# A matmul that reads its moving columns in turns from two halves

## The chip, the cores and the metric

The kernel runs on one core of one Trainium2 chip. The metric is the device time of one execution, in microseconds. Before the change the median of three runs is 925.33 us (925.14 to 925.72).

## The reference

One layer of a hybrid decoder block, float32, 512 tokens of 1024 channels. In short:

```
h    = RMSNorm(x);  proj = h @ w_in              # 1024 x 9216
y_a  = (B * conv3(C * v)) @ w_a_out              # B, C, v, u, ug, q, gates: columns of proj
y_b  = silu(LN(conv31(u * sigmoid(ug)))) @ w_b_out
y_c  = attention(q, RMSNorm(mem) @ w_kv) @ w_att_out     # 4 heads, 256 memory tokens
x    = x + (sum_i sigmoid(gate_i) * y_i) @ w_o
h2   = RMSNorm(x);  gt, up = split(conv3(h2 @ w_up))     # 1024 x 5632, causal, per channel
out  = RMSNorm(x + (silu(gt) * up) @ w_down)             # 2816 x 1024
```

The convolutions run along the tokens, each token using its predecessors.

## The kernel before, in words

Every product is made of three float32r matmuls: each operand is split into a high part (a ScalarE cast, line 495 for weights) and a low part (VectorE, line 499), and hi·hi, hi·lo and lo·hi are added up in PSUM.

The two large projections, `h @ w_in` and `h2 @ w_up`, go by quads. A quad makes 512 output channels (two tiles of 256) for all 512 tokens, by a Strassen-like scheme with seven products in place of eight: sums and differences of weight blocks (made by adding DMAs of GpSimd, line 633, or VectorE) meet sums and differences of the activations (`OPERAND`: b00, b10, b11, t4 to t7), which are kept as ready-split tiles of 128 partitions x 4 x 256 tokens. There are 18 quads in the mixer and 11 in the feed-forward part.

`multiply(q, f, act)` issues one product: 24 matmuls on line 675, two halves of 128 output channels, four blocks of 128 input channels, three terms each. The stationary operand is 128 x 128 of a weight, the moving one `a[k]`, 256 columns (tokens) that lie side by side. The result of 2 x 256 columns fills one PSUM bank. `quad_reads` empties the banks: `r1`, `r5`, `r6`, `r4` are ScalarE copies (r4 with a factor of -1), `r2`, `r7`, `r3` VectorE additions or subtractions into the quad's two output tiles `first` and `second`. In r5 the tile takes +b; in r7 `minus(t, x, y)` computes -x - y, so that -(a + b) stands there.

The other matmuls are not quads: keys (line 929, also 256 columns), attention, the merges of the three branches (lines 1417 to 1419), `w_o` and `w_down` (`product`, lines 446 to 448, mostly 512 columns).

The order of the work is planned when the program is built. `Jobs` holds every step as a job with an engine, a cost in us and what it needs. TensorE's jobs run in a list written out by hand. The jobs of ScalarE, VectorE, SP (weight loads) and GpSimd (adding DMAs) are put in order by a greedy clock that adds up the costs, with due times reckoned back from TensorE's list and corrections by hand (`LATER`, `AHEAD`). `MM`, `MM_HALF` and `MM_QUAD` in line 419 are the costs of a matmul of 512 columns, of 256 columns in some places, and of a quad's or a key's matmul; a product of a quad is booked at 24 x `MM_QUAD`. The engines then work through their own queues in that order, with semaphores between them. Weights pass through rings: six landing buffers `wf` and four pairs `whi`, `wlo`.

Of the kernel before, what the change touches and what calls it, by code (L numbers as in the profile page):

```python
# [10 lines left out]
AF = mybir.ActivationFunctionType  # L11
ALU = mybir.AluOpType
# [319 lines left out]
def hybrid_block_kernel(  # L332
# [19 lines left out]
    nc = tc.nc  # L352
# [27 lines left out]
    job = jobs.add  # L380
# [3 lines left out]
    def make(key, dtype=F32):  # L384

        ring, i = jobs.place[key]
        label = "_".join(str(k) for k in key) if isinstance(key, tuple) else key
        if ring == "ps":
            t = psum.tile([P, SEQ], F32, tag=f"ps{i}", name=name(str(key[0])))
        elif ring == "wf":  # L390
            t = wts.tile([P, 1024], F32, tag=f"wf{i}", name=name("wf"), bufs=1)
        else:
            t = places[ring].tile([P, 1024], dtype, tag=f"{ring}{i}", name=name(str(key[0])))
        tiles[key] = t
        return t

    def two(key):

        return tiles[key].rearrange("p (c n) -> p c n", c=2)
# [4 lines left out]
    def halves(key):  # L404

        return tiles[key].rearrange("p (c n) -> p c n", c=2)


    def dve(n):
        return (n + 151) / 960.0 - 0.08  # L410

    def actv(n):
        return (n + 224) / 1200.0 - 0.08
# [2 lines left out]
        return n / 1160.0 + 0.175 + extra  # L416

    TAP = 0.665
    MM, MM_HALF, MM_QUAD = 0.2268, 0.12, 0.1142
    LOAD, MORE, MORE_WIDE = 1.42, 2.55, 2.55  # L420
    LOAD_LATENCY, MORE_LATENCY = 3.1, 3.4

# [6 lines left out]
    cols, at = {}, 0  # L429
# [4 lines left out]
    def par(key, i):  # L434
        return pk[:, cols[key] + i : cols[key] + i + 1]
# [3 lines left out]
    nc.scalar.preload_act_table_set("sqrt_and_others")  # L439
    nc.scalar.dma_start(out=pk[:, :N_GAINS], in_=packed[:, :N_GAINS])  # L440
    nc.scalar.copy(mean_w, mean_col.broadcast_to([P, P]))

    def product(ps, w_hi, w_lo, s_hi, s_lo, start, stop, again=False):


        nc.tensor.matmul(ps, s_hi, w_hi, start=start, stop=False, skip_group_check=again)  # L446
        nc.tensor.matmul(ps, s_hi, w_lo, start=False, stop=False, skip_group_check=again)  # L447
        nc.tensor.matmul(ps, s_lo, w_hi, start=False, stop=stop, skip_group_check=again)  # L448

    def minus(t, x, y):  # L450

        nc.vector.scalar_tensor_tensor(t, x, -1.0, y, op0=ALU.mult, op1=ALU.subtract)
# [102 lines left out]
    lo_t, hi_t = slice(0, HALF), slice(HALF, SEQ)  # L555
# [107 lines left out]
    def multiply(q, f, act):  # L663
        if f in (1, 2, 5):
            make(("bank", q, BANK_OF[f]))
        ps = halves(("bank", q, BANK_OF[f]))
        (w_hi, w_lo), (hi, lo) = w_units.pop((q, f)), form[act, OPERAND[f]]
        for c in range(2):
            at = slice(c * P, (c + 1) * P)
            for i in range(4):  # L670
                k = 3 - i if f == 4 and c else i
                first = f in (1, 2, 5) and i == 0 and c == 0
                again = not (f in (1, 2, 5) and c == 0)
                for n, (w, a) in enumerate(((w_hi, hi), (w_hi, lo), (w_lo, hi))):
                    nc.tensor.matmul(  # L675
                        ps[:, c, :], w[:, k, at], a[k], start=first and n == 0,
                        stop=i == 3 and n == 2, skip_group_check=again,
                    )

    def multiply_job(q, f, act, unit=True):  # L680
        bank = ("bank", q, BANK_OF[f])
        after = [("wl", (q, f))]
        if (act, OPERAND[f]) in form_ready:
            after += form_ready[act, OPERAND[f]]
        else:
            after.append(("fl", act, OPERAND[f]))
        after += {6: [("r1", q)], 7: [("r6", q)], 4: [("r7", q)], 3: [("r5", q)]}.get(f, [])
        pe((q, f), 24 * MM_QUAD, lambda: multiply(q, f, act), after,
           take=[(bank, "ps")] if f in (1, 2, 5) else [], use=[] if f in (1, 2, 5) else [bank],
           unit=unit)  # L690
# [3 lines left out]
    def quad_reads(q, first, second, ring, after=()):  # L694

        f, s = lambda: two(first), lambda: two(second)
        bank = lambda b: ("bank", q, b)
        view = lambda b: halves(bank(b))

        def read1():  # L700
            make(first)
            nc.scalar.copy(f()[:, :, lo_t], view("a"))

        def read5():
            make(second)
            nc.scalar.copy(s()[:, :, hi_t], view("b"))

        def add(t, b):
            nc.vector.tensor_tensor(t, t, b, op=ALU.add)

        job(("r1", q), "ACT", actv(512), read1, [(q, 1)] + list(after),
            take=[(first, ring)], use=[bank("a")])
        job(("r2", q), "DVE", dve(512), lambda: add(f()[:, :, lo_t], view("c")),
            [(q, 2), ("r1", q)], use=[bank("c"), first])
        job(("r5", q), "ACT", actv(512), read5, [(q, 5)] + list(after),
            take=[(second, ring)], use=[bank("b")])
        job(("r6", q), "ACT", actv(512), lambda: nc.scalar.copy(f()[:, :, hi_t], view("a")),
            [(q, 6), ("r1", q)], use=[bank("a"), first])
        job(("r7", q), "DVE", dve(512), lambda: minus(s()[:, :, hi_t], view("a"), s()[:, :, hi_t]),
            [(q, 7), ("r5", q)], use=[bank("a"), second])  # L720
        job(("r3", q), "DVE", dve(512), lambda: add(f()[:, :, hi_t], view("b")),
            [(q, 3), ("r6", q)], use=[bank("b"), first])
        job(("r4", q), "ACT", actv(512), lambda: nc.scalar.activation(
            s()[:, :, lo_t], view("a"), AF.Copy, scale=-1.0), [(q, 4), ("r5", q)],
            use=[bank("a"), second])

    def ready_of(q, second):
# [307 lines left out]
    def mixer_quad(q, first, second, col0, col1):  # L1035
        quad_loads(q, w_in, col0, col1, by_dma=q != ("glu", 0), take=("wf+" + ANY, 6))
        quad_reads(q, first, second, ANY)
# [4 lines left out]
    for i in range(2):  # L1042
        a, b = 2 * i, 2 * i + 1
# [7 lines left out]
    for h in range(HEADS):  # L1051
# [18 lines left out]
        for tp in range(2):  # L1070
            at = ATT + 12 * h + 6 * tp
# [313 lines left out]
    for p in range(4):  # L1385
# [5 lines left out]
            lambda k, j, p=p: par("conv_a_w", k * KC + 2 * p + j), [("CV", p), ("ldp",)], ANY,  # L1391
# [347 lines left out]
    for q in range(QUADS):  # L1739
        up = ("up", q)  # L1740
        quad_loads(up, w_up, q * 256, D_FF + q * 256, by_dma=True,
                   **({"take": ("wf lf",), "after": [("fl", "h2", "t4")]} if 2 < q < 9 else {}))
        quad_reads(up, ("gt", q), ("uu", q), "tm",
                   ["temps"] + ([("z", q - 2)] if q > 1 else []))
        for value, src, acc in ((0, ("gt", q), ("gtc", q)), (1, ("uu", q), ("upc", q))):
            conv3_jobs(
                ("cf", q, value), src, acc,
                lambda k, j, q=q, v=value: par(
                    "conv_ffn_w", k * 2 * FC + v * FC + 2 * q + j),
                ready_of(up, value) + ([("z", q - 1)] if q else []), "tm",  # L1750
            )
        job(("silu", q), "ACT", actv(1024) + (0 if q else TABLE), lambda q=q: nc.scalar.activation(
            tiles["gtc", q], tiles["gtc", q], AF.Silu), [(("cf", q, 0), "done")],
            use=[("gtc", q)])
        job(("z", q), "DVE", dve(1024), lambda q=q: gated(q),
            [("silu", q), (("cf", q, 1), "done")], use=[("gtc", q), ("upc", q)])
# [112 lines left out]
    first = [(UP[0], 1), (UP[0], 2), "tr2", (UP[1], 1), "tr3", (UP[1], 2), (UP[2], 1), (UP[0], 5), (UP[2], 2), (UP[0], 6), (UP[1], 5), (UP[0], 7), (UP[0], 3), (UP[0], 4), (UP[1], 6), (UP[2], 5), (UP[1], 7), (UP[2], 6), (UP[1], 4), (UP[1], 3)]  # L1869
# [62 lines left out]
    for g, ps in enumerate(PIECES):  # L1932
        n = (ps.stop - ps.start) * HALF
        here = [("z", ps.stop - 1)]
        job(("zd", g), "DVE", dve(n), lambda ps=ps: z_difference(ps), here)
        for p, at in (("a", (0, 0)), ("b", (0, 1)), ("d", (0, 1)), ("c", (0, 0)), ("e", (0, 0)),
# [12 lines left out]
            k = down_pieces.index((p, g)) - 3  # L1949
# [46 lines left out]
    for u, ps in enumerate(PAIR_UNITS):  # L1996
        n = ps.stop - ps.start
# [239 lines left out]
```

## Time and profile before

| | |
|---|---|
| median of the runs | 925.33 us |
| span of the profiled execution | 923.8 us |
| TensorE matmuls | 916.6 us busy, 99%, 6677 matmuls |
| VectorE | 837.4 us, 91% |
| ScalarE | 671.0 us, 73% |
| GpSimd | 126.5 us, 14% |
| mean granted TensorE clock | 0.999 |

The page gives the span, from the first to the last instruction; the profiled execution has no other time of its own in it, and the runs' median lies 1.5 us above it. In the profile PE is TensorE, PEld its weight loads, DVE VectorE, ACT ScalarE, POOL GpSimd. Matmuls overlap in the pipeline, so the length of one (some 278 ns for 256 columns) is longer than the distance from one to the next; a busy TensorE does not say at which pace it works. The chain is followed back from the last instruction, at each step to what released it.

### The profile page before, as it was taken

What the parts mean: (1) busy time and instruction counts of PE and PEld (TensorE: products, weight loads), DVE (VectorE), ACT (ScalarE), POOL (GpSimd) and SP (SyncE); (2) the same over time, 40 slices, a digit from 0 to 9 for tenths busy, and PEclk for the clock granted to TensorE, in tenths of its full rate; (3) what the DMA queues carried; (4) which work ended last, traced back from release to release, by engine and by line L of the source; (5) the groups of instructions that cost most, each with busy time, mean ns of one, the idle gap of its engine ahead of it and who ended that gap; (6) DMA issues with size and microseconds to landing.
All of it is one profiled execution on the core that took longest, in us unless ns stands there. A gap on an engine that the chain in (4) does not pass through costs nothing.

```text
span 923.8 us, 16764 instructions
## 1 busy us (share of the span) xinstructions
PE 916.6 (99%) x6677; PEld 862.8 (93%) x6677; DVE 837.4 (91%) x953; ACT 671.0 (73%) x911; POOL 126.5 (14%) x153
## 2 busy tenths in 40 slices
PE   9999999999999999999999999999999999999997
PEld 8999999999989999999899888899999999988886
DVE  6897999989989999999986779898999889999987
ACT  7567988879977887788746743777766676765656
POOL 0121121101111211110100001021221121003300
PEclk9999999999999999999999999999999999999999
DMA  9999689666787879788956598499999877789962
GB/s 364 367 252 199 151 178 205 167 160 137 194 188 205 183 168 213 174 210 201 220 108 173 157 322 187 114 227 307 279 248 226 207 142 149 197 266 338 244 131 92
DMA packets 54366, 190.60 MB, mean 206 GB/s; under 512 B 6160, under 2 KB 6544, under 8 KB 54288
## 3 DMA queue, kind: packets, MB, share of 16 engines
q0 software_dynamic: 20880, 75.24, 45.2%
q1 hardware_dynamic: 33120, 114.02, 34.7%
q8 instruction: 52, 0.85, 0.3%
q10 hardware_dynamic: 288, 0.27, 0.1%
q14 instruction: 26, 0.21, 0.1%
HBM read 185.31 MB, written 4.19 MB: 205 GB/s over the span
## 4 chain that ended last, share of the span: by engine, by line
PE 95%; DMA 2%; DVE 1%; issue 0%; ACT 0%; POOL 0%; DVEq 0%; POOLq 0%; ACTq 0%
PE bank L675 57%; PE bank L448 7%; PE bank L446 7%; PE bank L447 7%; PE bank L1418 5%; PE bank L1417 5%; PE bank L1419 5%; PE bank L929 2%; DMA wf<-in_w_up 2%; PE bank L1766 0%; PE ss L802 0%; DVE wlo L499 0%; PE bank L1166 0%; DVE upc L1373 0%; DVE gtc L1373 0%
## 5 line engine op out<-in xcount | busy, mean ns | idle before, releaser
L495 ACT CAST whi<-wf 128x1024 fp32r<-128x1024 f32 (+1 forms) x199 | 206.9, 1044 | 97.7 <-PE bank L675 39.3
L499 DVE TENSOR_TENSOR wlo<-wf,whi 128x1024 fp32r<-128x1024 f32 (+1 forms) x193 | 232.4, 1211 | 29.8 <-ACT whi L495 29.6
L1238 ACT ACTIVATE tp<-u,pk 128x510 f32<-128x510 f32 (+22 forms) x184 | 119.4, 704 | 7.0 <-DVE acc L1245 6.9
L1245 DVE TENSOR_TENSOR acc<-acc,tp 128x1020 f32<-128x1020 f32 (+22 forms) x92 | 109.2, 1188 | 6.0 <-ACT tp L1238 5.0
L633 POOL DMA_DIRECT2D wf<-in_w_in x51 | 45.1, 890 | 245.1 <-DVE wlo L499 160.2
L675 PE MATMUL bank<-ft6h,wlo 128*128 128x256 f32 x232 | 64.3, 277 | 0.1
L675 PE MATMUL bank<-fb10h,whi 128*128 128x256 f32 x232 | 64.4, 278 | 0.0
L675 PE MATMUL bank<-fb00h,whi 128*128 128x256 f32 x232 | 64.4, 278 | 0.0
L675 PE MATMUL bank<-ft6h,whi 128*128 128x256 f32 x232 | 64.4, 277 | 0.0
L675 PE MATMUL bank<-ft7h,whi 128*128 128x256 f32 x232 | 64.3, 277 | 0.0
L675 PE MATMUL bank<-ft7l,whi 128*128 128x256 f32 x232 | 64.3, 277 | 0.0
L675 PE MATMUL bank<-ft7h,wlo 128*128 128x256 f32 x232 | 64.3, 277 | 0.0
L675 PE MATMUL bank<-fb00l,whi 128*128 128x256 f32 x232 | 64.3, 277 | 0.0
L675 PE MATMUL bank<-fb11h,whi 128*128 128x256 f32 x232 | 64.3, 277 | 0.0
L675 PE MATMUL bank<-fb00h,wlo 128*128 128x256 f32 x232 | 64.3, 277 | 0.0
L675 PE MATMUL bank<-ft5h,wlo 128*128 128x256 f32 x232 | 64.3, 277 | 0.0
L675 PE MATMUL bank<-ft5h,whi 128*128 128x256 f32 x232 | 64.3, 277 | 0.0
L675 PE MATMUL bank<-ft5l,whi 128*128 128x256 f32 x232 | 64.3, 277 | 0.0
L675 PE MATMUL bank<-ft6l,whi 128*128 128x256 f32 x232 | 64.2, 277 | 0.0
L675 PE MATMUL bank<-fb10h,wlo 128*128 128x256 f32 x232 | 64.2, 277 | 0.0
L675 PE MATMUL bank<-fb10l,whi 128*128 128x256 f32 x232 | 64.2, 277 | 0.0
L675 PE MATMUL bank<-fb11l,whi 128*128 128x256 f32 x232 | 64.1, 276 | 0.0
(388 smaller groups left out, 3146.1 us busy)
## 6 DMA issues: line engine op xcount, KB each, us to landing
wf<-in_w_in SPq DMA_DIRECT2D x55, 512.0 KB, 5.1
wf<-in_w_in POOLq DMA_DIRECT2D x51, 512.0 KB, 6.2
wf<-in_w_up SPq DMA_DIRECT2D x29, 512.0 KB, 5.7
wf<-in_w_up POOLq DMA_DIRECT2D x28, 512.0 KB, 6.1
wf<-in_w_down SPq DMA_DIRECT2D x15, 512.0 KB, 3.7
wf<-in_w_att_out SPq DMA_DIRECT2D x8, 512.0 KB, 4.5
wf<-in_w_a_out SPq DMA_DIRECT2D x8, 512.0 KB, 4.2
wf<-in_w_b_out SPq DMA_DIRECT2D x8, 512.0 KB, 4.3
```

The lines of the kernel that those rows point to most:

```text
L446: nc.tensor.matmul(ps, s_hi, w_hi, start=start, stop=False, skip_group_check=again)
L447: nc.tensor.matmul(ps, s_hi, w_lo, start=False, stop=False, skip_group_check=again)
L448: nc.tensor.matmul(ps, s_lo, w_hi, start=False, stop=stop, skip_group_check=again)
L495: nc.scalar.copy(parts[0], src())
L499: nc.vector.tensor_tensor(lo, src(), hi.bitcast(F32), op=ALU.subtract)
L633: nc.gpsimd.dma_start(out=tiles[key], in_=block(w, col[c], k), accum_op=ALU.add)
L675: nc.tensor.matmul(ps[:, c, :], w[:, k, at], a[k], start=first and n == 0, stop=i == 3 and n == 2, skip_group_check=again,)
L1238: nc.scalar.activation(two(("tp", p, s))[:, j, s:], two(("u", p))[:, j, : SEQ - s], AF.Copy, scale=weight(j),)
L1245: nc.vector.tensor_tensor(a, a, two(("tp", p, s))[:, :, s:], op=ALU.add)
L1417: nc.tensor.matmul(ps, w_hi[:, i, at], hi, start=first, stop=False)
L1418: nc.tensor.matmul(ps, w_hi[:, i, at], lo, start=False, stop=False)
L1419: nc.tensor.matmul(ps, w_lo[:, i, at], hi, start=False, stop=last)
```

## The change

The matmuls of the quads read their 256 columns in the order 0, 128, 1, 129, and so on: `in_turns` views the operand as two halves and takes a column from each in turn. The bank then holds the columns in that order, and its seven readers view it with `turned` (columns two apart, first the even ones, then the odd ones) and their tiles in SBUF with `parted` (two runs of 128), so that every token stands again where it stood. The readers' view needs one step more than the helper `minus` is given, so r7 becomes a plain subtraction, s - a, and r5 takes its bank with a factor of -1 in its place. The planner's cost of a quad's matmul is put at 0.1119 where it was 0.1142; the keys' matmuls, whose reading isn't changed, are booked at the same number.

```
-    MM, MM_HALF, MM_QUAD = 0.2268, 0.12, 0.1142
+    MM, MM_HALF, MM_QUAD = 0.2268, 0.12, 0.1119
...
+    def in_turns(t):
+        return t.rearrange("p (a b) -> p b a", a=2)
+
+    def turned(t):
+        if len(t.shape) == 3:
+            return t.rearrange("p c (b a) -> p c a b", a=2)
+        return t.rearrange("p (b a) -> p a b", a=2)
+
+    def parted(t):
+        if len(t.shape) == 3:
+            return t.rearrange("p c (a b) -> p c a b", a=2)
+        return t.rearrange("p (a b) -> p a b", a=2)
...
                     nc.tensor.matmul(
-                        ps[:, c, :], w[:, k, at], a[k], start=first and n == 0,
+                        ps[:, c, :], w[:, k, at], in_turns(a[k]), start=first and n == 0,
...
         def read1():
             make(first)
-            nc.scalar.copy(f()[:, :, lo_t], view("a"))
+            nc.scalar.copy(parted(f()[:, :, lo_t]), turned(view("a")))
         def read5():
             make(second)
-            nc.scalar.copy(s()[:, :, hi_t], view("b"))
+            nc.scalar.activation(
+                parted(s()[:, :, hi_t]), turned(view("b")), AF.Copy, scale=-1.0)
-        def add(t, b):
-            nc.vector.tensor_tensor(t, t, b, op=ALU.add)
+        def add(t, b, op=ALU.add):
+            nc.vector.tensor_tensor(parted(t), parted(t), turned(b), op=op)
...
-        job(("r6", q), "ACT", actv(512), lambda: nc.scalar.copy(f()[:, :, hi_t], view("a")),
+        job(("r6", q), "ACT", actv(512), lambda: nc.scalar.copy(
+            parted(f()[:, :, hi_t]), turned(view("a"))),
...
-        job(("r7", q), "DVE", dve(512), lambda: minus(s()[:, :, hi_t], view("a"), s()[:, :, hi_t]),
+        job(("r7", q), "DVE", dve(512), lambda: add(s()[:, :, hi_t], view("a"), ALU.subtract),
...
         job(("r4", q), "ACT", actv(512), lambda: nc.scalar.activation(
-            s()[:, :, lo_t], view("a"), AF.Copy, scale=-1.0), [(q, 4), ("r5", q)],
+            parted(s()[:, :, lo_t]), turned(view("a")), AF.Copy, scale=-1.0), [(q, 4), ("r5", q)],
```

Nothing else differs: the instructions, their number and TensorE's order stay, the orders of the other queues follow from the planner's cost.

## The prediction

> **What bounds the kernel now.** I read the page first (engines, the span in 40 slices, the chain), then the waits of TensorE, then the chain in order of time, then windows.
>
> ```profile
> span 923.8 us, 16764 instructions
> ...
> PE 916.6 (99%) x6677; PEld 862.8 (93%) x6677; DVE 837.4 (91%) x953; ACT 671.0 (73%) x911; POOL 126.5 (14%) x153
> ...
> PEclk9999999999999999999999999999999999999999
> ...
> PE 95%; DMA 2%; DVE 1%; issue 0%; ACT 0%; POOL 0%; DVEq 0%; POOLq 0%; ACTq 0%
> PE bank L675 57%; PE bank L448 7%; PE bank L446 7%; PE bank L447 7%; PE bank L1418 5%; PE bank L1417 5%; PE bank L1419 5%; PE bank L929 2%; DMA wf<-in_w_up 2%; PE bank L1766 0%; PE ss L802 0%; DVE wlo L499 0%; PE bank L1166 0%; DVE upc L1373 0%; DVE gtc L1373 0%
> ...
> L675 PE MATMUL bank<-fb00h,whi 128*128 128x256 f32 x232 | 64.4, 278 | 0.0
> ```
> ```profile
> PE bank L1766 <- POOL ident masks.py:199: 1.4, 1, 1.4
> ```
>
> TensorE is busy 99%, the chain is TensorE for 95%, and line 675, the quads' matmul that the change edits, alone carries 57%. The waits of TensorE hold one entry, 1.4 us at the start. The clock is granted in full throughout. So what counts is the pace at which line 675's matmuls follow each other. There are 29 quads of 7 products of 24 matmuls, 4872 in all (232 of each operand and part: 29 times 8). The mean of 278 ns is the life of one matmul in the pipeline, not its pace. The pace is read off the chain in order of time (start, length, count):
>
> ```profile
> 62.83 103.59 PE bank L675 x912
> ...
> 177.66 0.87 PE bank L1166 x8
> ...
> 182.14 2.73 PE bank L675 x24
> ...
> 187.61 2.83 PE bank L675 x24
> 193.15 5.65 PE bank L675 x48
> ...
> 285.83 153.12 PE bank L675 x1344
> ...
> 610.57 8.41 DMA wf<-in_w_up
> 619.54 11.44 DMA wf<-in_w_up x2
> ...
> 643.39 160.88 PE bank L675 x1414
> ```
> ```profile
> 43.70:166.40 122.70, 122.70 (x1059) 121.72 (x1058) 115.72 (x120) 98.54 (x131) 21.40 (x25) 1.00 0.88 203
> ...
> 243.00:285.00 42.00, 42.00 (x187) 34.76 (x187) 36.29 (x40) 33.20 (x49) 6.07 (x7) 1.00 0.78 182
> 286.00:362.00 76.00, 76.00 (x667) 76.00 (x666) 75.21 (x83) 63.12 (x88) 13.49 (x16) 1.00 0.81 190
> 362.00:438.00 76.00, 76.00 (x672) 76.00 (x671) 75.66 (x80) 61.28 (x84) 9.89 (x12) 1.00 0.83 197
> 438.00:471.00 33.00, 33.00 (x152) 27.46 (x151) 28.72 (x32) 20.50 (x28) 5.17 (x6) 1.00 0.82 188
> 599.00:643.00 44.00, 44.00 (x378) 43.83 (x376) 38.57 (x44) 33.15 (x46) 7.77 (x9) 1.00 0.99 263
> 643.00:804.00 161.00, 160.87 (x1415) 160.66 (x1415) 146.52 (x168) 112.85 (x141) 27.74 (x32) 1.00 0.88 208
> ```
> (Columns of the windows: the stretch, its length, then busy us of TensorE, its weight loads, VectorE, ScalarE and GpSimd, the clock, the DMA share, GB/s.)
>
> The long runs go at 103.59/912 = 113.6, 153.12/1344 = 113.9 and 160.88/1414 = 113.8 ns. Short ones differ for the very same instruction: 2.73/24 = 113.8, but 2.83/24 = 117.9 and 5.65/48 = 117.7. The matmuls of 512 columns of the window from 243 (its 187 count one or two that straddle an end) take 42.00/185, some 227 ns, twice the 113.6 of 256. So there is no fixed price of an instruction in it: the pace is a price per column, 0.443 ns, and the same instruction has two such prices. VectorE at 99% (286 to 438) or at 91% (643 to 804) doesn't move it. I read that as a pace set by how the operands are fetched, and this is what the change edits. Over all 4872: 3670 in the three long runs take 417.6 us; the other 1202 lie between 113.8 and 117.9, at the middle 139.3 us; together 557 us, 114.3 ns each.
>
> **The change, part by part.** *The order of the columns (line 675).* Same count of matmuls, same columns, same order of TensorE's instructions: the built programs show none moved on TensorE. What one costs when it alternates between two runs 128 columns apart, no row shows, since every moving operand of this kernel is read in one run. Bounds from the nearest rows: below, the fastest follow-on of a full instruction here, the transposes of line 1166, 0.87/8 = 109 ns (they stream half the columns, so this is a far row); above, the scores, 256 columns from another tile:
>
> ```profile
> 172.31 0.28 PE L447 MATMUL bank<-k,qh 128*128 128x256 f32 x1
> ...
> 174.47 0.28 PE L447 MATMUL bank<-k,qh 128*128 128x256 f32 x1
> ```
> 18 matmuls lie between these two starts, 2.16/18 = 120 ns. Further up stands the 227 of 512 columns, as if each column took two turns. I take 111.9. It lies near the middle of 109 and 114.3 (111.7), and the diff itself reprices a quad's matmul in the planner from 0.1142 to 0.1119 us; the old price is the 114.3 that I read off this trace, to 0.1 ns, so I take the new one as meant on the same scale. It is a claim of the edit and no measurement; hence the wide bounds. Gain: 4872 x 2.4 ns = 11.7 us, nearly all on the path.
>
> The Trainium skill, "TensorE: Matmul & The Clock Gate", section "Back-to-back issue gap", gives a warm gap of N/2.4 + 2.5 ns, 109.2 for 256 columns; the trace, at 113.6 and more, doesn't reach it. If the new order did, the gain by that page would be 4872 x 5.1 = 24.8 us, an estimate.
>
> *The readers.* Per quad four ScalarE reads (r1, r5, r6, r4) and three VectorE ones (r2, r7, r3) take the bank's columns two apart and write them in runs of 128.
>
> ```profile
> L709 DVE TENSOR_TENSOR gt<-gt,bank 128x512 f32<-128x512 f32 x22 | 15.0, 682 | 2.9 <-PE bank L675 2.9
> L452 DVE SCALAR_TENSOR_TENSOR uu<-bank,uu 128x512 f32<-128x512 f32 x11 | 7.5, 683 | 1.8 <-PE bank L675 1.8
> L1373 DVE SCALAR_TENSOR_TENSOR upc<-uu,pk,upc 128x511 f32<-128x511 f32 x22 | 16.4, 744 | 0.0
> L499 DVE TENSOR_TENSOR wlo<-wf,whi 128x1024 fp32r<-128x1024 f32 x190 | 230.3, 1219 | 29.1 <-ACT whi L495 28.9
> ...
> L723 ACT ACTIVATE uu<-bank 128x512 f32<-128x512 f32 x11 | 6.5, 588 | 0.0
> L706 ACT COPY uu<-bank 128x512 f32<-128x512 f32 x11 | 6.4, 580 | 0.9 <-PE bank L675 0.9
> ...
> L1673 DVE TENSOR_TENSOR fb11l<-bank,fb11h x2: 682/683/684, 607.5 to 611.6; 128x512 fp32r<-128x512 f32 x2
> ```
> Line 1673 already writes four runs of 128 from a bank in 683 ns, the time of line 709's two runs of 256: shorter runs cost nothing. The step of two has no row. VectorE's time is 682 ns for 512 elements and 1219 for 1024, whichever memory they come from, so 537 ns stream and 145 are fixed; I take the step as free (at 1.05 ns for an element from either memory the reader seems to move one at a time) and bound it above by a doubled stream, +537 ns on 87 VectorE reads. r7 becomes a two-operand subtract (683 to 682) and r5 an activation (580 to 588): 29 x 8 ns = 0.2 us of ScalarE, hidden by its 27% idle time.
>
> *The price in the planner.* It moves no computation, yet the hand-written clock behind ScalarE's, VectorE's, SP's and GpSimd's queues runs 2% faster in quads, so their orders change: conv taps, splits and reads trade places, a few GpSimd adds move (from the cv quads on), and SP's weight loads take other places in the ring. The diff has this from the price alone; the readers add no move. A load that slips costs TensorE its lateness; a queue that is better matched costs nothing. Between 0 and 3 us; I charge 0.5.
>
> *What is late next.* From 286 to 438 VectorE idles 0.8 + 0.3 = 1.1 us while TensorE would save 1339 x 2.4 = 3.2. VectorE there runs on taps not needed until the mean at 474, and from 438 to 471 it idles 4.3, so the cover (5.4) holds if the order lets it; I charge 1.0 of the 2.1. From 599 to 643 DMA is at 0.99 and the chain runs through the landings of w_up (8.41 and 11.44 us) into the ScalarE and VectorE steps behind them: what the 362 quad matmuls (the window's 378 less 16 transposes of rows) save there, 0.9 at 2.4 ns and 2.1 if they leave the pace of 117.8, is lost; I charge 1.5. In 643 to 804 VectorE idles 14.5, enough.
>
> **Sum.** 11.7 - 0.5 - 1.0 - 1.5 = 8.7 us off the span of 923.8, 915.1. The median of the runs, 925.33, lies 1.5 above the span; with that, 916.6. Own range: at 109 ns 25.8 less 2, 902; at 113.3 ns, with 3 us lost, 923.
>
> **The rivals.** *Two places per pair of columns cost more than one (slower).* The price per column changes for the same instruction, so fetching is at its limit; alternating asks for a new place at every column where one run asks for the next element. Decisive from 114.3 ns on. At the scores' 120 the time is 925.3 + 4872 x 5.7 ns = 953; if each column takes two turns (227), 925.3 + 549 = 1474. For it: the two prices for one instruction. Against it: those go with where the operands lie, not with order. The Trainium skill says so for memory: "SBUF — State Buffer", section "Specifications (TRN2)", has lines of 16 bytes that need two hits or more for full bandwidth; in turns, each fetch lands in another line than the one before. By that page this rival would be the forecast; no row here reads that way. Chance 0.15.
>
> *Readers twice as long.* With +537 ns on three VectorE reads a quad (1.61 us), the 8 quads of 286 to 438 need 12.9 us against 5.4 idle up to 471: 7.5 late. 43.7 to 166.4 (the run of 912, 5.4 quads, 8.7 us, against 7.0 idle less the 2.2 saved) 3.9 late; 643 to 804 (8.4 quads, 13.5 against 14.5 less 3.4) 2.4 late. 13.8 lost against 11.7 gained: 927. For it: VectorE at 99%. Against: one element at a time everywhere. Chance 0.07.
>
> *The order doesn't matter to the fetch.* The pace stays, the readers cost nothing, only the queues' orders differ: 924 to 927, most likely 925.5. For it: the two paces may come from where tiles lie, which stays. Chance 0.06.
>
> **How the numbers follow.** Forecast 0.72, the three rivals 0.15, 0.07 and 0.06. A measurement tells 0.2%, 1.9 us, from no change. Faster: the forecast and a little of the readers' case, 0.74; same: 0.06; slower: 0.20. The range takes in the forecast's 902 to 923, the case of no effect and the readers' 927 with 1 us to spare, and leaves the first rival out: 902 to 928; the forecast alone 902 to 923.
>
> **What would show it.** Right: the long runs of quad matmuls in the chain at 110 to 113 ns, quads' reads still at 680 and 580 ns, TensorE's waits still near nothing. Wrong: runs at 118 or more (first rival), reads over 900 ns with TensorE waiting for VectorE between 286 and 474 or after 643 (second), 113.8 again (third), or a new wait for w_up around 600 to 645 longer than 3 us.

## The result, and the profile after

The changed kernel takes 916.8 us (median of four runs, 916.76 to 918.41) against 925.24 for the kernel before, measured beside it: a ratio of 0.9911, 95% interval 0.9896 to 0.9925. The profiled execution has a span of 915.0 us, 8.8 less than before. Forecast were 916.6 and 915.1.

The page of the changed kernel, its engines, clock and chain:

```profile
span 915.0 us, 16771 instructions
...
PE 905.3 (99%) x6677; PEld 849.6 (93%) x6677; DVE 837.5 (92%) x953; ACT 668.5 (73%) x911; POOL 126.9 (14%) x153
...
PEclk9999999999999999999999999999999999999999
...
PE 89%; DVE 4%; DMA 4%; issue 2%; ACT 1%; SPq 0%; DVEq 0%; POOLq 0%; ACTq 0%
PE bank L691 53%; PE bank L463 6%; PE bank L464 6%; PE bank L462 6%; PE bank L1435 5%; PE bank L1437 5%; PE bank L1436 5%; DMA wf<-in_w_up 2%; PE bank L947 2%; DVE wlo L515 2%; DMA wf<-in_w_in 1%; DMA wf<-in_w_v 1%; DVE upc L1391 0%; PE ss L820 0%; DVE zl L1947 0%
```

The same instructions on TensorE, still 99% busy at a full clock, 11.3 us less of it. But the chain, 95% TensorE before, is 89% now: VectorE, ScalarE and the DMA have come into it. The pace is again read in the chain in order of time (start, length, what, count), line 691 being the quads' matmul:

```profile
62.94 101.84 PE bank L691 x912
...
185.76 2.68 PE bank L691 x24
...
282.61 133.94 PE bank L691 x1200
...
469.28 18.76 PE bank L691 x168
```

101.84/912, 2.68/24, 133.94/1200 and 18.76/168 are all 111.6 to 111.7 ns. The two prices of before (113.6 and 117.9 in the same kind of row) have become one: of the 4872 distances from a quad's matmul to the next, 4840 are 111 or 112 ns long.

The waits of TensorE (what waited, for whom; us in total, times, longest) were one row before, the start; now there are five:

```profile
PE bank L1784 <- POOL ident masks.py:199: 1.4, 1, 1.4
PE bank L464 <- DVE zl L1947: 1.0, 1, 1.0
PE bank L691 <- ACT gt L718: 0.8, 1, 0.8
PE bank L691 <- DVE wlo L515: 0.5, 1, 0.5
PE bank L463 <- DVE wlo L895: 0.2, 1, 0.2
```

Where the time went, from the starts of TensorE's matmuls in both traces, matched in their order: from the quads' matmuls to their successors 558.1 us before and 546.8 after, 11.3 less; from the 1319 matmuls of 512 columns 300.7 and 303.3, 2.6 more; the others 0.2 less. Together 8.8. Without waits the quads would have given 4872 x (114.30 - 111.66) = 12.9 us, the two means being those of the distances under 150 ns.

### The profile page after: what moved, and what is told of

Same layout as the page of the kernel before. It is cut to its first block, busy times and chain, and to the rows that moved or that the text cites. A ratio compares the mean times of both kernels' runs of the same rounds, so it can differ in the third digit from the quotient of the medians.

```text
span 915.0 us, 16771 instructions
## 1 busy us (share of the span) xinstructions
PE 905.3 (99%) x6677; PEld 849.6 (93%) x6677; DVE 837.5 (92%) x953; ACT 668.5 (73%) x911; POOL 126.9 (14%) x153
## 4 chain that ended last, share of the span: by engine, by line
PE 89%; DVE 4%; DMA 4%; issue 2%; ACT 1%; SPq 0%; DVEq 0%; POOLq 0%; ACTq 0%
PE bank L691 53%; PE bank L463 6%; PE bank L464 6%; PE bank L462 6%; PE bank L1435 5%; PE bank L1437 5%; PE bank L1436 5%; DMA wf<-in_w_up 2%; PE bank L947 2%; DVE wlo L515 2%; DMA wf<-in_w_in 1%; DMA wf<-in_w_v 1%; DVE upc L1391 0%; PE ss L820 0%; DVE zl L1947 0%
## 5 line engine op out<-in xcount | busy, mean ns | idle before, releaser
L511 ACT CAST whi<-wf 128x1024 fp32r<-128x1024 f32 (+1 forms) x205 | 212.4, 1043 | 93.1 <-PE bank L691 34.3
L515 DVE TENSOR_TENSOR wlo<-wf,whi 128x1024 fp32r<-128x1024 f32 (+1 forms) x199 | 239.5, 1211 | 25.6 <-ACT whi L511 25.2
L1263 DVE TENSOR_TENSOR acc<-acc,tp 128x964 f32<-128x964 f32 (+22 forms) x92 | 109.0, 1188 | 2.6 <-ACT tp L1256 0.7
L649 POOL DMA_DIRECT2D wf<-in_w_in x56 | 49.5, 884 | 265.5 <-DVE wlo L515 192.1
L691 PE MATMUL bank<-fb11h,wlo 128*128 128x256 f32 x232 | 63.8, 275 | 0.0
```

The lines of the kernel that those rows point to most:

```text
L511: nc.scalar.copy(parts[0], src())
L515: nc.vector.tensor_tensor(lo, src(), hi.bitcast(F32), op=ALU.subtract)
L649: nc.gpsimd.dma_start(out=tiles[key], in_=block(w, col[c], k), accum_op=ALU.add)
L691: nc.tensor.matmul(ps[:, c, :], w[:, k, at], in_turns(a[k]), start=first and n == 0, stop=i == 3 and n == 2, skip_group_check=again,)
L1263: nc.vector.tensor_tensor(a, a, two(("tp", p, s))[:, :, s:], op=ALU.add)
```

## The experiments

**What makes the pace: the order of the columns, the planner's price, or the place of the tiles?** Four kernels. The first is the kernel before with the new price alone, the second the change with the old price:

```
e1:  -    MM, MM_HALF, MM_QUAD = 0.2268, 0.12, 0.1142
     +    MM, MM_HALF, MM_QUAD = 0.2268, 0.12, 0.1119
e2:  -    MM, MM_HALF, MM_QUAD = 0.2268, 0.12, 0.1119
     +    MM, MM_HALF, MM_QUAD = 0.2268, 0.12, 0.1142
```

> The kernel before with nothing but the planner's price of a quad's matmul at 0.1119: the columns are read in one run, the queues of ScalarE, VectorE, SP and GpSimd stand in the order of the changed kernel. Theory A (the order in which the columns are fetched sets the pace): the long runs of quad matmuls stay at 113.3 to 113.9 ns and the slow products at 117.8, the time at 925 to 928. Rival B (the new order of the queues brings the gain): 915 to 919. Rival C (the gain is the vanishing of the slow pace alone, and that hangs on how the matmuls happen to follow the queues): the slow products of 117.8 go, 920 to 922.

> The changed kernel with the old price 0.1142 in the planner: columns read in turns, queues in the order of the kernel before. Theory A: every quad matmul at 111.7 ns, 914 to 918, with waits of TensorE between 1 and 5 us in other places than with the new price. Rival B: 925.

Measured: e1 927.32 us, ratio to before 1.0019 (1.0010 to 1.0027); e2 916.05 us, ratio 0.9900 (0.9886 to 0.9913). In e1 the quads' mean stays at 114.31 ns, in e2 it is 111.66. So the whole gain comes from the order of the columns. The price alone costs some 1.7 us; put together with the turns it makes no difference that these runs can tell (0.9911 against 0.9900, with intervals that overlap). Waits of TensorE in e1:

```profile
PE bank L448 <- DVE zl L1929: 0.9, 1, 0.9
PE bank L675 <- DVE wlo L499: 0.4, 1, 0.4
```

The price moved the queues of ScalarE and VectorE, and the split `zl` for `w_down` came late without any faster TensorE.

The next two take out `gap`, 16 columns (64 bytes) by which the last block of the tile t4 is set off, in the kernel before and in the changed one. What lies behind it moves with it, and nothing else is changed:

```
-            gap = (256 - SHIFT) // 4
+            gap = 0
```

> The kernel before without the gap of 16 columns (64 bytes) ahead of the last quarter of the t4 tile (that quarter's address moves by 64 bytes, nothing else). In the kernel before the products t4 hold the irregular distances (112 to 124 ns) behind which the slow pace of 117.8 turns into 113.3. Theory A with two paces by address: without the gap this turn is gone, the slow pace, once entered at 187 us, lasts through the long runs: some 4000 matmuls x 4.4 ns = 17 us more, about 942. Rival (the slow pace belongs to what other engines do at the time): 925, the same products slow as before.

> The changed kernel without that gap. Theory A (read in turns, the pace no longer hangs on the address): 111.7 ns throughout, 916 to 918. Rival C (the turns only help as long as the gap ends the slow pace): a pace of 116 or more in the long runs, 930 or more.

Measured: e3 931.31 us, ratio 1.0079 (1.0056 to 1.0103); e4 916.54, ratio 0.9904 (0.9890 to 0.9917). Three runs of quad matmuls in the chains, two of e3 and one of e4:

```profile
62.92 103.39 PE bank L675 x912
...
285.86 158.29 PE bank L675 x1344
```
```profile
283.01 150.08 PE bank L691 x1344
```

158.29/1344 = 117.8 ns in e3; before, the very same run took 153.12 us, 113.9. In e4 it is 111.67. Of the quads' distances 839 were 117 to 119 ns before, 2286 in e3. So a matmul that reads one run has a second, slower pace, and moving a tile by 64 bytes decides how many of them pay it; of the two kernels that read in turns, the changed one has a single such distance and e4 none.

The place alone doesn't set the pace, though. The earlier run of e3 reads the same tiles of the mixer at the same places as the later one, and goes at 103.39/912 = 113.4 ns. Product by product, the quads enter a stretch at 113 or at 118 ns and carry that pace on from product to product. In the kernel before, a slow stretch of the long runs ends within a product of t4, the tile with the gap (118 ns from 286 to 297 us, 113 from 300 to 438); without the gap it lasts to the end of the run (118 from 286 to 443). The expectation had this right, but put the cost at some 17 us where it is 5.6: the last long run of e3, from 649 us on, goes at 113. What starts a slow stretch was not tried.

**Which order is it?** Five kernels change only the view of the moving operand (in e9 by product; the readers stay, so the tokens come out in other places):

```
     -        return t.rearrange("p (a b) -> p b a", a=2)
e5:  +        return t.rearrange("p (a b e) -> p b a e", a=2, e=2)
e6:  +        return t.rearrange("p (a b e) -> p b a e", a=2, e=4)
e7:  +        return t.rearrange("p (a b) -> p b a", a=4)
e8:  +        return t.rearrange("p (b a) -> p a b", a=2)
e9:  +    near = {1: 64, 2: 32, 5: 16, 6: 8, 7: 4}     # two single columns in turn, so far apart
     +        if f in near:
     +            return t.rearrange("p (h a b) -> p h b a", a=2, b=near[f])
     +        if f == 3:
     +            return t.rearrange("p (a b e) -> p b a e", a=2, e=16)
     +        return t
```

> The changed kernel, but the matmul takes two columns from each half in turn (0, 1, 128, 129, ...). The readers are left as they are, so the tokens of a pair stand permuted in the output; the work is the same. Theory A1 (what costs is each passage to a new stretch of some 64 bytes, and two streams that pass together share part of it): 111 to 112 ns, 915 to 918. Rival A2 (what costs is each change of place, so single columns in turn pay most): lower than 111.7, about 110, 908 to 911.

> As with the pairs, but four columns (16 bytes) from each half in turn; tokens permuted in the output, same work. Theory A1: 111 to 112 ns, 915 to 918. Rival A2: lower still than with pairs, 109 to 110, 905 to 909. A third way: with a whole line of 16 bytes at a time it reads like one run, 113.3 ns, 923 to 925.

> The columns in turns from four quarters (0, 64, 128, 192, 1, ...); tokens permuted in the output, same work. Theory A1: four streams share the passages, 110 to 111.5 ns, 909 to 916. Rival A2: 111.7 or more, since each column changes place as now: 917.

> The columns with a stride of two in the matmul (0, 2, 4, ..., 1, 3, ...), one stream that passes each stretch twice; tokens permuted in the output, same work. Theory A1: twice as many passages as in one run, 118 to 121 ns, 945 to 965. Rival A2: each column in another place than the one before but two of them in a line of 16 bytes, 111 to 114 ns, 915 to 927.

The same run of 1344 in the chains of e5, e6, e7 and e8:

```profile
357.62 221.09 PE bank L691 x1344
```
```profile
303.95 170.34 PE bank L691 x1344
```
```profile
327.34 192.47 PE bank L691 x1344
```
```profile
449.82 308.12 PE bank L691 x1344
```

Pairs from each half 164.5 ns (1177.8 us in all), fours 126.7 (987.1), single columns from four quarters in turn 143.2 (1067.3), every second column and then the others 229.3 (1488.6). These are paces and not waits: the longest wait of TensorE behind the start is 0.8 us in each of them. Both theories with which I went in missed these numbers. What they do show: turns as such are no gain, and the form of the change, two streams and one column from each, is the only one of these five (the four and the change's own) that beats one run.

> The changed kernel with another reading order for each of the seven products, all in the same run: two streams in turns whose places lie 64 columns apart (b00), 32 (b10), 16 (t5), 8 (t6) and 4 (t7); runs of 16 columns from each half in turn (b11); one run (t4). Tokens stand permuted in the output, the work is the same. Theory S (the pattern's shape decides: two single columns in turn are cheap at any distance, longer inner runs or more streams are not): b00 to t7 all at 111 to 113 ns, b11 above 113.3, t4 at 113.3 or 117.8. Theory D (the distance decides: two places can be served together only where they lie far enough apart): 111.7 down to some distance, then 140 to 229 for the near ones, as with the columns two apart; b11 about 115, since it changes place 16 times.

Measured: 926.08 us. The five products that take single columns in turn at distances of 64, 32, 16, 8 and 4 columns all follow at 111.6 to 111.7 ns; the product with 16 columns from each half at 120.2; t4, left in one run, at 113 and 118, mean 117.5. From 4 columns to 128 the distance of the two streams makes no difference that shows here (the later runs find a floor of 111.7 ns under every matmul, so a smaller price would not show); the form does.

The Trainium skill, "SBUF — State Buffer", section "Specifications (TRN2)", asks for two or more hits in a line of 16 bytes for full bandwidth. These runs don't bear it out for the moving operand: e8 takes two columns of a line one after the other and pays 229 ns, e6 takes whole lines and pays 126.7, and the change itself, which goes to another line at each column, pays 111.7. Why pairs, fours and four streams cost what they cost stays open.

**Why 111.7, and what is left?** Two explanations: the price per column in turns is 111.7/256, or something that belongs to each matmul and not to its columns takes 111.7. The next kernel reads every matmul in turns, those of 512 columns and the keys too, with the readers adapted as in the change:

```
     def product(ps, w_hi, w_lo, s_hi, s_lo, start, stop, again=False):
+        w_hi, w_lo = in_turns(w_hi), in_turns(w_lo)
...
-                         ps[:, j, :], w[:, k, at], a[:, k, :],
+                         ps[:, j, :], w[:, k, at], in_turns(a[:, k, :]),
...
+                hi, lo = in_turns(hi), in_turns(lo)
...
-                row, row, tiles["bank", "wo", wo_bank(p), t],
+                parted(row), parted(row), turned(tiles["bank", "wo", wo_bank(p), t]),
```

> The changed kernel with the same reading in turns in the other matmuls too: keys, scores, values, attention output, merges, w_o and w_down, all of 256 or 512 columns, their readers adapted in the same way. Theory: the price per column of the turns, 0.436 ns, holds at 512 columns (two places 256 columns apart): 223.3 in place of 226.7 to 233, 111.7 in place of 113 to 120; about 1300 matmuls x 3.3 to 9 ns, 5 to 7 us less than the changed kernel, 909 to 913. Rival (the gain is one of the distance of 128 columns): 226 or more at 512, 915 to 918. Rival (VectorE's and DMA's stretches take it back): paces fall as said, the time stays at 914 to 917.

Measured: 906.29 us, ratio 0.9784 (0.9771 to 0.9798), less than the 909 to 913 that the price per column promised. The 512-column matmuls follow at 216 ns where 223.3 was expected (227 before), the keys and other 256-column ones at 111.6 (116.4), the quads at 111.66 as in the change. 216 for 512 is 0.422 ns a column, so 256 columns would need 108.0. They take 3.7 more. A stretch of e10 in which all matmuls have 512 columns (columns as in the prediction's windows):

```profile
237.00:277.00 40.00, 40.00 (x187) 35.01 (x187) 38.78 (x43) 34.60 (x52) 6.04 (x7) 1.00 0.85 217
```

As many matmuls, 187 with those that straddle an end, fill 42.00 us in the prediction's window from 243, where 40.00 do here. The Trainium skill, "TensorE: Matmul & The Clock Gate", section "Back-to-back issue gap", gives N/2.4 + 2.5 ns for a matmul without the cost of its weight load, 215.8 for 512: in turns the trace agrees, in one run it doesn't (227), and for 256 columns (109.2) neither does.

The same page of the Trainium skill says that the spacing of pairs of weight load and matmul is set by both, so the weight load was the suspect: each matmul here has its own, of 128 x 128. The next kernel narrows four products and leaves the loads as they are:

```
+    WIDTH = {6: 240, 7: 224, 4: 192, 3: 224}
...
-                        ps[:, c, :], w[:, k, at], in_turns(a[k]), start=first and n == 0,
+                        ps[:, c, : WIDTH.get(f, 256)], w[:, k, at],
+                        a[k][:, :224] if f == 3 else in_turns(a[k][:, : WIDTH.get(f, 256)]),
+                        start=first and n == 0,
```

> The kernel after with fewer columns in some of a quad's products: product 6 takes 240 columns in turns, product 7 224 in turns, product 4 192 in turns, product 3 224 in one run; products 1, 2 and 5 keep 256 in turns. The last columns of those four products are left out of the result. Theory W (each matmul brings a weight load of 128x128, and the loads can't follow each other faster than about 111.7 ns): all seven products stay at 111.5 to 111.8 ns whatever their width, the one run of 224 too, and the time stays at that of the kernel after, 914 to 919 us. Rival C (in turns the pace is a price per column, 111.67/256 = 0.436 ns; in one run 113.33/256 = 0.443 ns): 104.7 ns at 240, 97.7 at 224, 83.8 at 192, 99.2 at 224 in one run; each product has 29 times 24 = 696 matmuls, so the quads take 696 x (7.0 + 14.0 + 27.9 + 12.5) = 42.7 us less before waits; with VectorE at over 90% much of it would turn into waits, 885 to 910 us.

Measured: 918.96 us. A long run of its chain, in which all widths take part:

```profile
282.71 123.52 PE bank L693 x1104
```

123.52/1104 = 111.9. By product: 111.6 ns at 240 columns, 111.1 at 224, 110.7 at 192, and 111.6 for 224 in one run, which by columns would need 99.2. A quarter of the columns less, and the same pace: it is a floor under each pair of load and matmul. That the load sets it is what the trace of before speaks for, in a place that I hadn't read: line 802, sums of squares in float32, whose matmuls have a moving operand of one column and a load of 128 x 128 each. Its loads and its matmuls in the timeline of before (start, length, engine, count):

```profile
19.98 0.75 PEld L802 LDWEIGHTS ss<-mean_col,msq 128*128 128x128 f32 x6
```
```profile
20.10 0.72 PE L802 MATMUL ss<-mean_col,msq 128*128 128x1 f32 x6
```

The second of these matmuls starts 26 ns after the first. From there on, one column each, they start 111 or 112 ns apart, and so do the loads: six loads of 192 ns in 0.75 us are (750 - 192)/5 = 112. One matmul can follow another in 26 ns, but behind that first pair these keep to the pace of their loads, 112. e11 has the same in its quads: where 192 columns come behind a product of 256, the second of them follows the first in 85 ns, and from there on they go at 111 or 112. The same page of the Trainium skill, section "LDWEIGHTS (loading the stationary operand)", has P/1.2 ns for P columns of weights, 106.7 here; the runs show 111.7. So far as tried, then, a matmul of this kernel takes the longer of two times: its load's 111.7, or its columns at 0.422 ns in turns and 0.443 to 0.46 in one run. Transposes of line 1166 and their loads, at 109 ns, lie a little under the first; that was not followed up. A kernel with fewer loads was not tried, so that it is the load and not something else of the pair is read from the traces and not tested by a run.

The last kernel is e10 with the planner told the measured paces:

```
-    MM, MM_HALF, MM_QUAD = 0.2268, 0.12, 0.1119
+    MM, MM_HALF, MM_QUAD = 0.216, 0.1117, 0.1117
```

> The version that reads every matmul's moving operand in turns, with the planner told the paces measured there: 0.216 us for 512 columns (0.2268 before), 0.1117 for 256 (0.12 and 0.1119). The matmuls are the same, so their paces stay at 216 and 111.3 to 111.7 ns. Only the queues' orders change. By the runs with one price changed (1.7 us slower in the one, 0.8 us faster in the other direction) I expect 903 to 909 us, most likely 906, the same as without the new prices. Rival: the planner's clock, right for the first time, removes the waits that the version without it has (1.2, 1.2, 1.1, 1.0 and 1.0 us are its longest), and the time falls to 899 to 902.

Measured: 902.79 us (902.06 to 903.51), ratio 0.9755 (0.9742 to 0.9769), the fastest of all. The paces are those of e10 (216.3 and 111.67), so the 3.5 us against it are the queues' order. The longest waits of TensorE behind the start, e10 first (its profile is of the longest of its five executions, 908.45 us), then e12:

```profile
PE bank L463 <- ACT zh L1945: 1.2, 1, 1.2
PE bank L463 <- DVE x L1652: 1.2, 1, 1.2
PE bank L692 <- DVE ft6l L618: 1.1, 1, 1.1
PE bank L465 <- DVE zl L1952: 1.0, 1, 1.0
PE bank L1678 <- DVE xnorm L1670: 1.0, 1, 1.0
```
```profile
PE bank L692 <- DVE wlo L516: 0.7, 2, 0.5
PE bank L692 <- ACT gt L735: 0.7, 1, 0.7
PE bank L464 <- DVE wlo L516: 0.6, 1, 0.6
```

I had put 906 and 903 as the lowest; it came out just below, short of the rival's 902, and for the rival's reason: of the 1.0 to 1.2 us waits none is left. With e1 and e2 this says that a right price isn't worth a fixed sum. In e1 it was wrong for the pace at hand and cost 1.7 us; here three prices became right together and gave 3.5.

## Why the prediction was right, point by point

**The pace (11.7 us).** Right in mechanism and nearly in size: 111.66 where I took 111.9, 12.9 us in place of 11.7. Of this, 4872 x (113.33 - 111.67) = 8.1 us is the step from the one-run price to the floor, and 4872 x (114.30 - 113.33) = 4.7 is the second, higher price of some matmuls, which went away whole. The reading "a price per column, set by how the operands are fetched" fits before (113.3 ns for 256 columns, 227 for 512) and the 512 columns of e10. It isn't the whole for 256 columns: there the change leads onto the weight load's floor, which my bounds of 109 and 120 didn't name, though line 802 of before had it. That row could have given 111.7 as the least that the change can reach. My 111.9 rests on no row of such a read: it is the edit's price in the planner, which lies near the middle of my bounds, and that it came so near is luck as far as my reading goes. The lower end of 902, 109 ns, was out of reach for this change.

**The readers (0).** Right. VectorE's and ScalarE's reads of the changed kernel (count, shortest/median/longest ns, first and last start):

```profile
L726 DVE TENSOR_TENSOR gt<-gt,bank x22: 677/680/689, 618.8 to 811.2; 128x512 f32<-128x512 f32 x22
```
```profile
L718 ACT COPY gt<-bank x11: 576/581/621, 602.9 to 784.5; 128x512 f32<-128x512 f32 x11
```

680 and 581 ns, as before. The step of two in a bank is free, and the rival that doubled it falls.

**VectorE from 286 to 438 (1.0 charged).** The place was right and the size near: at 427 one matmul comes 790 ns after the one before it, 0.7 us late. The cause was another than a full VectorE. Windows of the changed kernel (columns as in the prediction's):

```profile
362.00:438.00 76.00, 75.48 (x654) 74.48 (x654) 74.57 (x79) 59.76 (x82) 9.54 (x11) 1.00 0.85 206
438.00:471.00 33.00, 33.00 (x168) 28.08 (x167) 26.94 (x30) 17.82 (x24) 6.08 (x7) 1.00 0.82 179
599.00:643.00 44.00, 43.18 (x383) 42.67 (x382) 39.04 (x42) 31.98 (x42) 9.54 (x11) 1.00 1.02 267
```

VectorE idles 1.4 us from 362 to 438, and TensorE 0.5. The chain there:

```profile
416.55 0.59 DVE g L726
417.14 1.29 DVE acc L1248 x2
418.44 1.15 DVE wlo L515
...
419.60 6.03 DMA wf<-in_w_in
...
425.70 1.05 ACT whi L511
...
426.78 1.24 DVE wlo L515
...
428.06 5.40 PE bank L691 x46
```

Two convolution steps stand ahead of a weight's split on VectorE; the split frees a landing buffer, and only then does the next load start, 6.03 us long, and its cast and split end after TensorE has come. A late split costs by the load behind it.

**The DMA from 599 to 643 (1.5 charged).** Too much. The DMA is at 1.02, and at 634.8 one matmul comes 1041 ns after the one before it, 0.9 us late, since ScalarE's cast of a weight that had landed late stands ahead of the bank's read:

```profile
623.80 9.45 DMA wf<-in_w_up
...
634.24 1.04 ACT whi L511
635.28 0.49 ACT gt L718
```

But the matmuls ahead of that gained more than it took. The lead over before, from matmul to matmul, is 6.5 us at 600 and 7.7 at 637, and with the stop behind it 7.3 at 643 (times of before): 0.8 gained in the stretch, where my charge left between -0.6 and 0.6.

**The planner's queues (0.5 charged), and what I missed.** The largest loss stands at the step into `w_down`, at 821 to 823, for which I had charged nothing by itself. Behind the last product of the quads VectorE has its read, taps, product and splits to do before TensorE can go on:

```profile
818.29 1.21 DVE wlo L515
819.50 1.14 DVE z L1753
820.64 0.60 DVE wlo L515
821.24 0.33 DVE z L468
...
822.31 0.94 DVE zl L1947
```

Three distances between matmuls of 512 columns are 503, 339 and 1401 ns there, 227, 227 and 263 before, and the lead over before falls from 10.4 us to 8.8. The lead itself is not the cause, since the last product of the quads comes as much earlier. The other runs tell two causes apart. From the start of VectorE's last read of the quads (`gt`, line 726) to the start of this `zl` pass 10.1 us with the old price in the planner (before and e2) and 11.1 with the new one (the changed kernel, e1, e5 and e8), at whatever pace TensorE goes: 1.0 us is the new order's. e5 to e8, whose TensorE comes to this place 60 to 560 us later than before, all wait 0.8 us for `zl`. The rest, some 0.6, is the faster pace's: the read starts 0.95 us after the last quad matmul has started (1.07 in e2), where it was 0.35 before.

In sum: charged 0.5 + 1.0 + 1.5 = 3.0, found 12.9 - 8.8 = 4.1, of which 0.7, 0.9 and 1.5 stand in the three places and the rest in small pieces. The underestimated gain (1.2) and the underestimated losses (1.1) cancel; that is luck, and the forecast is nearer than its steps.

**The rivals.** "Two places per pair of columns cost more than one" is wrong for the change, and its price wasn't out of the world: e8 pays 229 ns, the rival's 227, for a step of two within one run. My argument against it, that the two prices go with where the operands lie, doesn't hold as it stands: e3 shows both prices on the same tiles at the same places. "The order doesn't matter to the fetch" falls with e2: the price taken back, the gain stays.

## What to carry to other kernels

Ask of each matmul which of two times is the longer, its columns or its weight load, and look for the row that shows each alone: here a matmul of one column showed the load's 112 ns and a matmul of 512 the columns'. An edit to the columns pays down to the load's time and no further, here 2.6 ns for 256 columns (and some 11 for 512), so the larger gain lay in the matmuls that the change left alone. And when a saturated engine gets faster, or the order of the other queues changes, look at the steps from one stage to the next, where a chain of work behind the last product has nothing to hide it: the 1.0 us that the new order put into that chain was lost at every pace of TensorE. Tell the planner the new pace of everything that changed.

## What was not expected of the hardware

A float32r moving operand read in one run costs 0.443 ns a column, and in some stretches 0.46 with the very same tiles, a pace that goes on from one matmul to the next; read in turns from two streams, one column each, it costs 0.422 (512 columns, streams 256 apart). With 256 columns, streams 4 to 128 columns apart all come down to the 111.7 ns of the floor. Two columns from each stream (164.5 ns for 256), four (126.7), sixteen (120.2), four streams (143.2) and a step of two (229.3) all cost more than one run. No run here says why.
